# Gate rows of the matrix memory prepared two tiles ahead, and the weight sums of the down-projection issued behind the bank's sum

## The chip, the cores and the metric

The kernel runs on one core of a Trainium2 chip. The metric is the device time of one execution in microseconds. Before the change it is 2307.58 us, the median of 3 runs (2306.45 to 2310.1).

## What is computed

One encoder layer over 2048 prompt tokens and 128 sample tokens, D_MODEL = 1024, all in float32. A combined input projection feeds two groups of heads, an mLSTM matrix memory (4 heads of 128) and a sliding-window attention; their outputs go through one output projection and a norm, and a gated convolutional feed-forward network with D_FF = 2816 follows. Cut to what the change touches:

```python
def trunk_layer(x, pos, C0, n0, m0, k_cache, v_cache, conv_prev, mchunk, w_in, ...):
    qm, km, vm, om, ip, fp, qa, ka, va = split_in(x @ w_in)
    ...
    hm, C1, n1, m1 = mlstm_chunkwise(qm, km, vm, logi, logf, C0, n0, m0, mchunk)
    hm = (og * head_norm(hm, g_mlstm_norm)).reshape(B, T, M_WIDTH).astype(x.dtype)
    ...
    mix = jnp.concatenate([hm, ha], axis=-1) @ w_out
    h = layer_norm(DEEPNORM_ALPHA * x + mix, ln1_g, ln1_b)
    f, conv_rows = conv_ffn(h, conv_prev, w_up, w_conv, b_conv, w_down)
    y = layer_norm(DEEPNORM_ALPHA * h + f, ln2_g, ln2_b)

def step(carry, inp):          # of mlstm_chunkwise, one chunk
    C, n, m = carry
    b = jnp.cumsum(lf, axis=-1)
    inter = b + m[..., None]
    dmat = jnp.where(causal, b[..., :, None] - b[..., None, :] + li[..., None, :], -jnp.inf)
    mt = jnp.maximum(inter, jnp.max(dmat, axis=-1))
    w_inter = jnp.exp(inter - mt)
    s = jnp.einsum('bhld,bhsd->bhls', qc, kc) * jnp.exp(dmat - mt[..., None])
    num = w_inter[..., None] * jnp.einsum('bhld,bhde->bhle', qc, C) + jnp.einsum('bhls,bhse->bhle', s, vc)
    ...
```

## The kernel before

The work is cut into tiles of 128 tokens: 16 of the prompt (0 to 15) and one of the sample. It runs in four stages: the input projection (up to about 640 us), the output projection (to about 940 us), the up-projection of the feed-forward network (to about 1840 us) and the down-projection. The dense products of all stages use a fast matrix product with seven products for eight (Strassen's), so a product is named (b, g, s): block of tiles b, group of columns g, step s of the seven. Every fp32 operand is split into a high and a low half, and three matmuls are made for one.

In the input projection a product (b, g, s) fills one of three PSUM banks A, B and C. Behind it `i_after` empties banks: ACT copies A or B into a tile `zev` (L813, L816, L824), and in steps 5 and 4 the inner function `add` makes DVE add bank C to `zev` (L828 or L830): "the bank's sum". The next product into a bank cannot begin before its copy is done. The order of steps in a block is 1, 7, 6, 2 and then, for a group, 5, the next group's 1, 3, 4, then the next group's 6, 7, 2.

Between the dense products, two chains run tile by tile from about 280 us on: the matrix memory (`m_chain`) and the attention (`a_chain`). They are generators. `Chains.weave` advances a planned clock by the cost of each dense piece and steps a chain when its planned time has come: `yield cost, wait, banks` says how much TensorE time the step took, how long to stay away, and how many of the five rotating PSUM banks (`bank`) must be planned free. This fixes the order of TensorE's instructions. The order on DVE, ACT, POOL and SP is made by a scheduler from the order in which the program issues them and its own estimates; `issue_after(x)` puts what is issued under it behind `x` on x's engine. Each engine works through its list strictly in order.

Steps of one tile t of the matrix memory, with their lines before the change:

- `m_rows(t)`: two transposes of the gates into a bank `pgr` (L1057, L1058), then seven small DVE instructions on 4 partitions: two scans (`r_b` L1136, `r_M` L1138), `ay` L1137 and L1068, the row `nmrow` (L1140, L1141) and `mc` L1144.
- `m_spread(t, 0)` writes the row to memory (`zrow<-nmrow`, L1150); `m_spread(t, 1)` reads it back to all 128 partitions (`nm<-zrow`, L1153). Both are DMAs on SP's queue.
- `m_tile`: `m_cols` transposes `ay` (bank `pcol`) and copies it to `col` (L1079); `m_masked` makes `dt` from `nm` (L1175); `m_emt` (L1084); `m_inter`, four exponentials of `nm` to the weights `wi` (L1187); `m_exps`, four of `dt` (L1181); scores; `sd` (L1198), `kw` (L1272); then the banks `pnum` (L1282) and `pcu` (L1290).
- `m_norm`: statistics and `hn` on DVE (L1222), then `mr`, three instructions on `mq` (L1225 to L1227), and a power on POOL (L1228). `m_scaled`: `ms` on DVE (L1233) and four scalings of `hn` on ACT (L1235). `m_out`: four transposes of `hn` into the bank `pht` (L1245).

Before the change the rows of tile t+1 are made inside tile t, right behind its columns, and spread in its next two steps. `m_inter` depends on `nm` alone.

`d_sums(k, step)` prepares sums of the down-projection's weights, eight times in the second half of the input projection and three times in the output projection: step 0 loads two tiles `txy<-wdn` (L897, L898), step 1 makes four DVE subtractions on them (L903 to L906), step 2 stores them (`zt<-txy`, L908, L909).

Of the kernel before, what the change touches and what calls it, by code (L numbers as in the profile page):

```python
# [10 lines left out]
AF = mybir.ActivationFunctionType  # L11
# [193 lines left out]
class Prog:  # L205
# [416 lines left out]
    def i_dense(self):  # L622
# [18 lines left out]
        for q in (2, 4):  # L641
            for _ in range(2 + (q == 2) * 2):
# [18 lines left out]
        passages = [{1: ["load"], 7: ["t3", 7], 6: ["t2", 6], 3: [3, "t4"], 4: ["b12", "t1"]},  # L661
                    {1: ["load"], 6: ["t3"], 7: [7, "t2"], 5: [6], 3: [3, "t4"], 4: ["b12", "t1"]}]
        sums = 0
        after = None
        for item in self.items:
            if after:

                after[0] -= 1
                if after[0] == 3:
                    self.logs_of(after[1] - 1)  # L670
                if after[0] < 0:
                    self.i_done = after[1]
                    after = None
            self.chains.hold = item[0] == "t" and item[1] > 0
            if item[0] == "t":
                _, b, ti, e = item
                if ("g", e, 3) not in self.wu:
                    self.advance()
                if b not in self.gates:
                    self.gates[b] = self.tp.tile([P, 5, 8], F32, name="gates", tag="gates", bufs=2)  # L680
                ps = self.bank([P, 512], "pg") if ti == 4 or e < 0 and ti % 2 == 0 else self.ib[ti % 2 * 2]
                yield from self.i_direct(b, ti, e, ps)
                self.i_keys(b, ti, ps)
                if ti == 1 and b:
                    if b + 1 < nb:
                        self.x_steps(b + 1, 1, 2)
                    else:
                        self.release(4)
                    after = [6, b + 1]
                elif ti == 3 and b or ti == 4:  # L690
                    self.release(4)
                elif item in begin:
                    self.x_steps(0, *begin[item])
                    for e in self.x_room.values() if ti == 2 else ():
                        e[1] = True
                if ti == 3 and b or ti == 4:
                    self.x_steps(b, 4)
                    if b:
                        self.x_steps(b, 5)
                self.advance()  # L700
                continue
            _, b, g, s = item
            if item not in self.wu:
                self.advance()
            yield from self.i_product(b, g, s)
            del self.wu[item]
            self.release(2)
            if self.trans and s != 4:
                self.i_transposes()
            behind = self.i_after(b, g, s)  # L710
            if (b, g, s) == (0, 0, 7):
                self.t_setup()
            if b and (g, s) == (1, 6):
                self.rope_load(IBLOCKS[b][0], 2)
            if g == last and b + 1 < nb:
                if s == 7:
                    self.rope_load(IBLOCKS[b + 1][2], 2)
                for x in passages[b > 0].get(s, ()):
                    if x == "load":
                        self.spare = True  # L720
                        self.x_load(b + 1, 1, 2, 3, 4)
                    else:
                        self.x_steps(b + 1, x)
            if (b, g, s) == (0, last, 4):
                self.x_steps(1, 1, 2)
                after = [6, 1]
            if g == last and b + 1 == nb and s in (7, 5, 2, 3):
                self.x_pair(0, (7, 5, 2, 3).index(s))
            with self.tc.issue_after(behind) if behind and b == 0 else nullcontext():
                self.advance()  # L730
                self.x_steps(0, *begin.get(item, ()))
                if item == ("p", 0, 0, 2):
                    self.x_single(4)

            if b >= nb // 2 and g < last:

                steps = (6, 2, 5) if g == last - 1 else (6, 5, 3)
                if s in steps:
                    self.d_sums(sums, steps.index(s))
                    sums += s == steps[2]  # L740
        self.sums = sums
        self.logs_of(nb - 1)
        self.chains.hold = False
# [77 lines left out]
    def i_after(self, b, g, s):  # L821
# [3 lines left out]

        def add(u):
            if g < 2:
                V.scalar_tensor_tensor(u, C, KSCALE, u, op0=ALU.mult, op1=ALU.add)  # L828
            else:
                V.tensor_add(u, C, u)  # L830
        if s == 1 and g == 0:
            return nc.scalar.copy(B, A).ins
        elif s == 6:
# [247 lines left out]

    def m_emt(self, col):
        emt = self.work("emt", [P, MH], bufs=2)
        self.nc.scalar.activation(emt, col[:, 36:40], AF.Exp)  # L1084
        return emt

    def place(self, t, blocks=IBLOCKS):
# [8 lines left out]
    def m_chain(self):  # L1096
# [3 lines left out]
        pend = None  # L1100
        self.rows = {}
        there = lambda t: t < NPT and self.i_done > self.place(t)[0]
        for t in range(NPT):
            while not there(t):
                yield 0, 500
            if pend is None:
                self.m_rows(t)
                self.m_spread(t, 0)
                self.m_spread(t, 1)
# [4 lines left out]
            hn = self.m_norm(*(yield from self.m_tile(t, *pend, *self.rows.pop(t))))  # L1114
            pend = None
            yield 950, 3000, 1
            self.m_scaled(hn)
            if there(t + 1):
                if t + 1 not in self.rows:
                    self.m_rows(t + 1)  # L1120
                    self.m_spread(t + 1, 0)
                    self.m_spread(t + 1, 1)
                pend = self.m_load(t + 1, *self.place(t + 1)),
            yield 150, 6800, 1
            self.m_out(t, hn[0])
            self.chains.done["m"] = t
        nc.sync.dma_start(self.a["m_p"], self.mc)
        nc.sync.dma_start(self.a["cn_p"], self.C)

    def m_rows(self, t):  # L1130
# [14 lines left out]
        self.rows[t] = [i, nm]  # L1145

    def m_spread(self, t, step):
        nc, z = self.nc, self.zrow[t]
        if step == 0:
            self.behind_pe(nc.sync.dma_start(z.rearrange("o (h m) -> (o h) m", h=MH), self.rows[t][1]))  # L1150
            return
        self.rows[t][1] = nm = self.work("nm", [P, MH, 129], bufs=2)
        self.behind_pe(nc.sync.dma_start(nm.rearrange("p h m -> p (h m)"), z.to_broadcast([P, MH * 129])))  # L1153

    def m_load(self, t, b, ti):
# [95 lines left out]
    def m_tile(self, t, load, i, nm):  # L1251
# [3 lines left out]
        col = self.m_cols(i)  # L1255
        with self.tc.issue_after(self.colcopy.ins):
            dt = self.m_masked(nm[:, :, :P], self.mcau)
        ahead = t + 1 < NPT and self.i_done > self.place(t + 1)[0]
        if ahead:
            self.m_rows(t + 1)  # L1260
        yield 330, 2800
        emt = self.m_emt(col)
        wi = self.m_inter(nm)
        self.m_exps(dt, col)
        yield 0, 5000, 2
        if ahead:
# [5 lines left out]
        V.tensor_mul(kw, kt, dt[:, :, P - 1:P].to_broadcast([P, MH, P]))  # L1272
        nc.gpsimd.tensor_mul(qk[:, 0:4], qk[:, 0:4], wi)
# [953 lines left out]
```

## Time and profile before

| | us |
|---|---|
| median of 3 runs | 2307.58 |
| the profiled execution, its own time | 2307.89 |
| its span in the trace | 2305.7 |
| TensorE (PE) busy | 2266.6 |
| VectorE (DVE) busy | 1808.2 |
| ScalarE (ACT) busy | 1306.8 |
| GpSimd (POOL) busy | 225.5 |

The matmul engine is busy almost throughout, so the time is read from the places where it isn't: a row of the timeline gives start, duration, engine, line, output<-input, and in square brackets the idle time of the engine before it with what ended that. A row of the view of waits gives who waited for whom, the total in us, the number of times and the longest. The 2.2 us between the profiled execution's time and its span lie outside the trace.

### The profile page before, as it was taken

To read this page: it belongs to the slowest core of one execution; us is meant where nothing else is said; L and a number is where in the kernel's file an instruction comes from. 1 tells how busy PE (TensorE), PEld (TensorE's weight loads), DVE (VectorE), ACT (ScalarE), POOL (GpSimd) and SP (SyncE) were. 2 spreads that over 40 slices of the span, in tenths; PEclk is the share of its full clock that TensorE was granted. 3 is DMA by queue.
4 is the path that set the end of the run, shared out by engine and by line. 5 is a ranking of instruction groups with operands and counts; after the bars stand their busy time and mean duration, and the time that the engine had idled before them with its cause. 6 is when DMAs were issued, how large, how long until landed. Compare 5 with 4: busy or idle time off the path is not lost.

```text
span 2305.7 us, 39752 instructions
## 1 busy us (share of the span) xinstructions
PE 2266.6 (98%) x14329; PEld 2086.1 (90%) x14329; DVE 1808.2 (78%) x3157; ACT 1306.8 (57%) x2465; POOL 225.5 (10%) x289
## 2 busy tenths in 40 slices
PE   8999999999999999999999999999999999999998
PEld 8999989898887778999999999999999988888887
DVE  8777686787789888987788666778766787796897
ACT  5453466676765665555556455555554644654753
POOL 0001001101122121200002000002000000000100
PEclk9999999999999999999999999999999999999999
DMA  7898999899986767787777889888998786656753
GB/s 279 299 322 287 297 308 328 295 303 332 320 278 237 241 220 248 282 322 282 275 270 263 282 309 322 308 305 270 328 292 260 240 286 225 240 196 225 242 188 110
DMA packets 299797, 629.23 MB, mean 273 GB/s; under 512 B 47373, under 2 KB 140625, under 8 KB 299601
## 3 DMA queue, kind: packets, MB, share of 16 engines
q1 hardware_dynamic: 298736, 623.55, 79.1%
q10 hardware_dynamic: 864, 3.15, 0.4%
q8 instruction: 113, 1.85, 0.3%
q14 instruction: 84, 0.68, 0.1%
HBM read 456.01 MB, written 170.59 MB: 272 GB/s over the span
## 4 chain that ended last, share of the span: by engine, by line
PE 78%; DVE 10%; DMA 6%; ACT 3%; issue 2%; SPq 0%; POOL 0%; DVEq 0%; ACTq 0%; POOLq 0%
PE dps L1931 18%; PE fup L1931 18%; PE dps L758 11%; PE dps L2135 6%; PE fht L2135 6%; PE fup L2135 5%; PE dps L232 2%; PE dps L233 2%; PE dps L234 2%; DMA txy<-wdn 2%; DVE w L228 2%; PE dps L783 1%; DMA w<-zws 1%; PE psx L767 1%; PE ppo L1420 1%
## 5 line engine op out<-in xcount | busy, mean ns | idle before, releaser
L1931 PE MATMUL dps<-hh,uw 128*128 128x384 f32 (+1 forms) x1848 | 477.5, 327 | 5.4 <-DVE u L1964 2.6
L1931 PE MATMUL fup<-hh,uw 128*128 128x384 f32 (+1 forms) x1848 | 476.4, 326 | 0.0
L1979 DVE SCALAR_TENSOR_TENSOR cc<-u,cw,cc 128x768 f32<-128x768 f32 (+1 forms) x264 | 257.7, 978 | 125.0 <-ACT cc L1977 121.6
L1931 PEld LDWEIGHTS dps<-hh,uw 128*128 128x128 f32 x1848 | 329.2, 188 | 7.9 <-DVE u L1964 3.2
L1931 PEld LDWEIGHTS fup<-hh,uw 128*128 128x128 f32 x1848 | 329.3, 188 | 0.0
L1931 PE MATMUL fup<-hl,uw 128*128 128x384 f32 (+1 forms) x924 | 301.3, 326 | 0.2 <-DVE hl L228 0.2
L1931 PE MATMUL dps<-hl,uw 128*128 128x384 f32 (+1 forms) x924 | 301.0, 326 | 0.0
L758 PE MATMUL dps<-w,oh 128*128 128x256 f32 x1344 | 252.1, 283 | 4.6 <-DMA w<-zws 2.2
L758 PEld LDWEIGHTS dps<-w,oh 128*128 128x128 f32 x1344 | 210.1, 188 | 17.1 <-issue 9.3
L228 DVE TENSOR_TENSOR w<-wraw,w 128x1024 fp32r<-128x1024 f32 (+1 forms) x155 | 185.8, 1202 | 50.4 <-ACT w L227 48.0
L227 ACT CAST uw<-wraw 128x1024 fp32r<-128x1024 f32 x126 | 123.2, 981 | 173.4 <-PE dps L2135 104.1
L227 ACT CAST w<-wraw 128x1024 fp32r<-128x1024 f32 (+1 forms) x155 | 155.0, 1005 | 88.9 <-PE dps L758 44.3
L228 DVE TENSOR_TENSOR uw<-wraw,uw 128x1024 fp32r<-128x1024 f32 x126 | 142.5, 1131 | 63.9 <-ACT uw L227 63.8
L758 PE MATMUL dps<-w,ol 128*128 128x256 f32 x672 | 187.2, 279 | 0.0
L1977 ACT ACTIVATE cc<-u,cw 128x768 f32<-128x768 f32 (+1 forms) x132 | 131.9, 1000 | 95.6 <-DVE u L1973 92.6
L758 PE MATMUL dps<-oh,w 128*128 128x256 f32 x896 | 167.0, 282 | 7.8 <-ACT zev L824 3.9
L1931 PEld LDWEIGHTS fup<-hl,uw 128*128 128x128 f32 x924 | 173.5, 188 | 1.1 <-DVE hl L228 1.1
L1931 PEld LDWEIGHTS dps<-hl,uw 128*128 128x128 f32 x924 | 173.5, 188 | 0.0
L2135 PE MATMUL fup<-uw,fu 128*128 128x512 f32 x726 | 169.3, 389 | 0.1
L2135 PEld LDWEIGHTS fup<-uw,fu 128*128 128x128 f32 x726 | 136.1, 188 | 28.7 <-ACT fht L2142 0.5
L2135 PE MATMUL dps<-uw,fu 128*128 128x512 f32 x660 | 160.9, 389 | 0.1
L758 PEld LDWEIGHTS dps<-oh,w 128*128 128x128 f32 x896 | 139.7, 188 | 14.1 <-ACT zev L824 4.5
(346 smaller groups left out, 4563.6 us busy)
## 6 DMA issues: line engine op xcount, KB each, us to landing
uw<-zw SPq DMA_DIRECT2D x176, 512.0 KB
zw<-uw SPq DMA_DIRECT2D x88, 512.0 KB
w<-zws SPq DMA_DIRECT2D x72, 512.0 KB
wv<-wup SPq DMA_DIRECT2D x66, 512.0 KB
wraw<-wi SPq DMA_DIRECT2D x62, 512.0 KB
wraw<-zt SPq DMA_DIRECT2D x60, 512.0 KB
wraw<-wdn SPq DMA_DIRECT2D x45, 512.0 KB
wraw<-wo SPq DMA_DIRECT2D x40, 512.0 KB
```

What stands on the lines that cost most here:

```text
L227: nc.scalar.copy(hi, src)
L228: nc.vector.tensor_sub(lo, src, hi.bitcast(F32))
L232: mm(out, ah, bh, start=start, stop=False)
L233: mm(out, ah, bl, start=False, stop=False)
L234: self.mark = mm(out, al, bh, start=False, stop=stop)
L758: self.mark = mm(o, l, r, start=s in (1, 7) and c == k == i == 0, stop=k == 3 and i == 2, skip_group_check=True)
L767: mm(o, x[:, k], w[:, k], start=s == 1 and k == i == 0, stop=s in (2, 4) and k == 3 and i == 2, skip_group_check=True)
L783: mm(o, x, w, start=k == i == 0, stop=k == KD - 1 and i == 2, skip_group_check=True)
L1931: mm(ps, l[:, k], r[:, k], start=s in (1, 7) and k == 0 and i == 0, stop=k == 3 and i == 2, skip_group_check=True)
L1977: S.activation(c[:, v], u[:, v, 2:2 + n], AF.Identity, bias=w[3], scale=w[2])
L1979: V.scalar_tensor_tensor(c[:, v], u[:, v, i:i + n], w[i], c[:, v], op0=ALU.mult, op1=ALU.add)
L2135: mm(ps, l[:, k, c], r[:, k], start=s in (1, 4, 7) and u == 0 and k == 0 and i == 0, stop=u == nu - 1 and k == n - 1 and i == 2, skip_grou ...
```

## The change

The rows of tile t+2 are now made at the end of tile t, behind `m_scaled`; their write to memory is issued behind `m_out(t)`, and the read back to all partitions in the middle of tile t+1, behind `m_exps`. A flag in `self.rows` says whether the row has been spread. A tile whose rows are not there yet gets them at once, as before (`at_once`). `m_inter` is put behind `emt`, so the weights come behind the columns. The planned cost of the step after `m_cols` goes from 330 to 180. `d_sums` follows a table: the load one or more products earlier or at the same product, the subtractions mostly one product later (at step 1 of the next group) and behind the last bank's sum.

```diff
+        sum_at = {(0, 7): 0, (1, 1): 1, (0, 3): 2, (1, 6): 0, (2, 1): 1, (1, 3): 2,
+                  (2, 6): 0, (3, 1): 1, (2, 3): 2, (3, 6): 0, (3, 2): 1, (3, 5): 2}
...
-            if b >= nb // 2 and g < last:
-
-                steps = (6, 2, 5) if g == last - 1 else (6, 5, 3)
-                if s in steps:
-                    self.d_sums(sums, steps.index(s))
-                    sums += s == steps[2]
+            if b >= nb // 2 and (g, s) in sum_at:
+                step = sum_at[g, s]
+                with self.tc.issue_after(self.added.ins):
+                    self.d_sums(sums, step)
+                sums += step == 2
...
         def add(u):
             if g < 2:
-                V.scalar_tensor_tensor(u, C, KSCALE, u, op0=ALU.mult, op1=ALU.add)
+                self.added = V.scalar_tensor_tensor(u, C, KSCALE, u, op0=ALU.mult, op1=ALU.add)
             else:
-                V.tensor_add(u, C, u)
+                self.added = V.tensor_add(u, C, u)
...
+        def at_once(t):
+            if t not in self.rows:
+                self.m_rows(t)
+                self.m_spread(t, 0)
+                self.m_spread(t, 1)
...
             self.m_scaled(hn)
             if there(t + 1):
-                if t + 1 not in self.rows:
-                    self.m_rows(t + 1)
-                    self.m_spread(t + 1, 0)
-                    self.m_spread(t + 1, 1)
+                at_once(t + 1)
                 pend = self.m_load(t + 1, *self.place(t + 1)),
+            ahead = there(t + 2) and t + 2 not in self.rows
+            if ahead:
+                self.m_rows(t + 2)
             yield 150, 6800, 1
             self.m_out(t, hn[0])
+            if ahead:
+                self.m_spread(t + 2, 0)
...
         with self.tc.issue_after(self.colcopy.ins):
             dt = self.m_masked(nm[:, :, :P], self.mcau)
-        ahead = t + 1 < NPT and self.i_done > self.place(t + 1)[0]
-        if ahead:
-            self.m_rows(t + 1)
-        yield 330, 2800
+        yield 180, 2800
         emt = self.m_emt(col)
-        wi = self.m_inter(nm)
+        with self.tc.issue_after(self.emtcopy.ins):
+            wi = self.m_inter(nm)
         self.m_exps(dt, col)
+        if t + 1 in self.rows and not self.rows[t + 1][2]:
+            self.m_spread(t + 1, 1)
         yield 0, 5000, 2
-        if ahead:
-            self.m_spread(t + 1, 0)
...
         yield 950, 4000, 4
-        if ahead:
-            self.m_spread(t + 1, 1)
```

How it moves instructions is seen in the engines' lists. (In the change's list, line numbers are higher by 1 to 7: L1194 is the old L1187, L1240 the old L1233.) ACT's list at the end of tile 0, before:

```order
L816 COPY zev<-dps 128x512
L1187 ACTIVATE wi<-nm 128x128 x4
L227 CAST w<-wraw 128x1024
L1235 ACTIVATE hn<-hn,ms 128x128 x4
L824 ACTIVATE zev<-dps 128x512
L1415 COPY pth<-ppt 128x512 x2
```

The same place now:

```order
L817 COPY zev<-dps 128x512
L1242 ACTIVATE hn<-hn,ms 128x128 x4
L825 ACTIVATE zev<-dps 128x512
L227 CAST w<-wraw 128x1024 x2
L1418 COPY pth<-ppt 128x512 x2
```

The four weights of tile 1 stood between two copies of banks and ahead of tile 0's `hn`; now they stand further down, behind the columns of their own tile:

```order
L1085 ACTIVATE emt<-col 128x4
L853 COPY dps<-dps 128x512
L1430 COPY mixa<-ppo 128x512
L1194 ACTIVATE wi<-nm 128x128 x4
L1188 ACTIVATE dt<-dt,col 128x128 x4
```

DVE's list at the norm of tile 0 (`mq`, `ms`) and the second set of weight sums (`txy`), before:

```order
L1225 TENSOR_TENSOR mq<-bmv,mr 128x4
L1226 TENSOR_TENSOR mq<-mq,mr 128x4
L1227 TENSOR_SCALAR mq<-mq 128x4
L903 TENSOR_TENSOR txy<-txy 128x512
L1233 TENSOR_TENSOR ms<-ms,mr 128x4
L228 TENSOR_TENSOR w<-wraw,w 128x1024
L904 TENSOR_TENSOR txy<-txy 128x512
L828 SCALAR_TENSOR_TENSOR zev<-dps,zev 128x512
```

The same place now; `txy` is the first set of sums here:

```order
L1232 TENSOR_TENSOR mq<-bmv,mr 128x4
L1233 TENSOR_TENSOR mq<-mq,mr 128x4
L1143 SCALAR_TENSOR_TENSOR r_b<-pgr,k_seg 4x128
L1234 TENSOR_SCALAR mq<-mq 128x4
L1144 TENSOR_TENSOR ay_765<-pgr,r_b 4x128
L1240 TENSOR_TENSOR ms<-ms,mr 128x4
L1145 SCALAR_TENSOR_TENSOR r_M<-k_seg,mc,ay_765 4x128
L1147 TENSOR_SCALAR nmrow<-r_M 4x128
L1069 SCALAR_TENSOR_TENSOR ay_765<-r_b,r_M 4x128
L1151 TENSOR_TENSOR mc<-r_b,r_M 4x1
L1143 SCALAR_TENSOR_TENSOR r_b<-pgr,k_seg 4x128
L1148 COPY nmrow<-mc 4x1
```

The rows of tile 1 and of tile 2 now stand in and behind the tail of tile 0's norm, ahead of the bank's sum L829 and of the four subtractions, which follow it. All four subtractions of the earlier set, which stood some forty rows higher among the attention's reductions, have moved down to here.

More of the change, by code (lines that the diff above doesn't have):

```diff
@@ L1083, in m_emt @@
         emt = self.work("emt", [P, MH], bufs=2)
-        self.nc.scalar.activation(emt, col[:, 36:40], AF.Exp)
+        self.emtcopy = self.nc.scalar.activation(emt, col[:, 36:40], AF.Exp)
         return emt
@@ L1106, in m_chain @@
             if pend is None:
-                self.m_rows(t)
-                self.m_spread(t, 0)
-                self.m_spread(t, 1)
+                at_once(t)
                 pend = self.m_load(t, *self.place(t)),
@@ L1113, in m_chain @@
                 yield 0, 1000, 2
-            hn = self.m_norm(*(yield from self.m_tile(t, *pend, *self.rows.pop(t))))
+            hn = self.m_norm(*(yield from self.m_tile(t, *pend, *self.rows.pop(t)[:2])))
             pend = None
@@ L1144, in m_rows @@
         V.tensor_add(self.mc, bc[:, P - 1:P], M[:, P - 1:P])
-        self.rows[t] = [i, nm]
+        self.rows[t] = [i, nm, False]
     def m_spread(self, t, step):
@@ L1151, in m_spread @@
             return
-        self.rows[t][1] = nm = self.work("nm", [P, MH, 129], bufs=2)
+        self.rows[t][1:] = nm, _ = self.work("nm", [P, MH, 129], bufs=2), True
         self.behind_pe(nc.sync.dma_start(nm.rearrange("p h m -> p (h m)"), z.to_broadcast([P, MH * 129])))
```

## The prediction

> **What bounds the kernel now.** First the busy time of the engines by stretch; the columns are start and end, length, busy us of PE, PEld, DVE, ACT and POOL, the granted clock, the share of the DMA engines and GB/s. The change touches the stretch from 310 us, where the chains run beside the input projection, to 940 us.
>
> ```profile
> 310.00:640.00 330.00, 318.52 (x2636) 291.12 (x2635) 248.47 (x756) 231.14 (x606) 37.46 (x36) 0.99 0.93 316
> 640.00:940.00 300.00, 297.37 (x1630) 236.46 (x1630) 265.21 (x609) 186.28 (x443) 71.81 (x43) 1.00 0.72 240
> ```
>
> PE is busy for 318.52 of 330 us and for 297.37 of 300. No matmul is removed, so all there is to win is PE's idle time, 11.5 + 2.6 = 14.1 us, 0.6% of the run. Next, what PE waited for in the first stretch, then in the second:
>
> ```profile
> PE dps L758 <- ACT zev L824: 3.7, 3, 2.5
> PE dps L783 <- DVE zev L830: 2.1, 1, 2.1
> PE dps L758 <- DMA w<-zws: 0.9, 2, 0.8
> PE dps L758 <- ACT zev L816: 0.9, 1, 0.9
> PE pnum L1282 <- DVE sd L1198: 0.9, 1, 0.9
> PE dps L758 <- DVE zev L830: 0.8, 1, 0.8
> PE pgr L1057 <- ACT pth L1415: 0.8, 1, 0.8
> ...
> PE pht L1245 <- ACT hn L1235: 1.7, 2, 1.0
> ```
>
> Most of it is a bank not emptied in time (L816, L824, L830). ACT and DVE have time to empty it on average, 231 and 248 us of 330; they are late where their lists stand still. Why they do, from their own waits in the first stretch:
>
> ```profile
> ACT wi L1187 <- DMA nm<-zrow: 20.7, 7, 5.1
> ACT sc L1386 <- DVE amx L1379: 17.7, 10, 2.6
> DVE ms L1233 <- POOL ms L1228: 8.6, 8, 1.7
> DVE txy L903 <- DMA txy<-wdn: 6.5, 5, 2.3
> DVE txy L904 <- DMA txy<-wdn: 4.5, 2, 3.9
> ```
>
> ACT stands 20.7 us for `nm` and DVE 11.0 us for `txy`. These are the change's targets. But 31.7 us of standing lists cost PE little: the timeline shows where. PE first, then ACT and DVE.
>
> ```profile
> 314.20 0.49 PE L1282 MATMUL pnum<-v,sd 128*128 128x129 f32 x2 [0.87 <-DVE sd L1198]
> 319.23 0.39 PE L758 MATMUL dps<-oh,w 128*128 128x256 f32 x1 [0.67 <-ACT zev L824]
> 323.15 0.39 PE L758 MATMUL dps<-oh,w 128*128 128x256 f32 x1 [0.92 <-ACT zev L816]
> 330.14 0.39 PE L758 MATMUL dps<-oh,w 128*128 128x256 f32 x1 [2.55 <-ACT zev L824]
> ...
> 325.97 1.28 ACT L1187 ACTIVATE wi<-nm 128x128 f32<-128x128 f32 x4 [2.87 <-DMA nm<-zrow]
> 328.33 1.28 ACT L1235 ACTIVATE hn<-hn,ms 128x128 f32<-128x128 f32 x4
> 329.52 0.58 ACT L824 ACTIVATE zev<-dps 128x512 f32<-128x512 f32 x1
> ...
> 322.50 0.83 DVE L1222 SCALAR_TENSOR_TENSOR hn<-pnum,bmv,og 128x128 f32<-128x128 f32 x3
> 325.08 0.17 DVE L1227 TENSOR_SCALAR mq<-mq 128x4 f32<-128x4 f32 x1
> 327.53 0.69 DVE L903 TENSOR_TENSOR txy<-txy 128x512 f32<-128x512 f32 x1 [2.29 <-DMA txy<-wdn]
> 328.14 0.15 DVE L1233 TENSOR_TENSOR ms<-ms,mr 128x4 f32<-128x4 f32 x1
> ```
>
> Around 330 us both targets meet: ACT waits for `nm` to 325.97, then for `ms`, which stands on DVE behind a subtraction that waits for `txy` to 327.53. Only then comes `hn`, and behind it the copy L824 for which PE has stood 2.55 us. The four gaps make 0.87 + 0.67 + 0.92 + 2.55 = 5.0 us. The other place is at 410 us:
>
> ```profile
> 409.85 0.69 DVE L904 TENSOR_TENSOR txy<-txy 128x512 f32<-128x512 f32 x1 [3.92 <-DMA txy<-wdn]
> 414.77 0.39 PE L758 MATMUL dps<-w,oh 128*128 128x256 f32 x1 [0.73 <-ACT zev L813]
> 419.67 0.38 PE L758 MATMUL dps<-w,oh 128*128 128x256 f32 x1 [0.52 <-ACT zev L824]
> ```
>
> DVE stands 3.92 us, the columns behind it come late, ACT's exponentials too, and with them two copies: 1.25 us on PE.
>
> **The change part by part.** One row of the grouped view for each kind carries the durations of `d_sums` and `m_rows` (count, total us, mean ns, idle before):
>
> ```profile
> L903 DVE TENSOR_TENSOR txy<-txy 128x512 f32<-128x512 f32 x11 | 7.5, 683 | 6.5 <-DMA txy<-wdn 6.5
> L1138 DVE TENSOR_TENSOR_SCAN r_M<-k_seg,mc,ay 4x128 f32<-4x128 f32 x14 | 6.9, 490 | 0.3
> L1136 DVE TENSOR_TENSOR_SCAN r_b<-pgr,k_seg 4x128 f32<-4x128 f32 x14 | 5.7, 404 | 0.0
> L1068 DVE SCALAR_TENSOR_TENSOR ay<-r_b,r_M 4x128 f32<-4x128 f32 x14 | 3.9, 281 | 0.3
> L1137 DVE TENSOR_TENSOR ay<-pgr,r_b 4x128 f32<-4x128 f32 x14 | 3.8, 274 | 0.2
> L1140 DVE TENSOR_SCALAR nmrow<-r_M 4x128 f32<-4x128 f32 x14 | 3.0, 213 | 0.3
> ```
>
> A set of four subtractions is 4 x 0.68 = 2.7 us of DVE. The rows of a tile are 0.49 + 0.40 + 0.28 + 0.27 + 0.21 = 1.65 us, and some 1.9 with the two on 4x1, which I take at 0.14 each as an estimate below the 0.21. Nothing of it is added or removed; all of it moves.
>
> *At 313 to 330 us: -4.1.* The first set of sums moves behind the bank's sum, so three of its subtractions (2.0 us) no longer stand ahead of `sd`. DVE reaches `sd` at about 311.4 instead of 313.46, before PE wants it: 0.87 goes. ACT follows DVE there (it waited 17.7 us for `amx` in ten places), so its copies come up to 2.0 us earlier, more than 0.67 and than 0.92: both go. At the last gap, `mq` (its last instruction ended at 325.25) ends 2.7 us earlier and, with `r_b` (0.40) ahead of it, at 322.9; the weights are out of the way. From there to the end of a free power on POOL is 1.1 us (to 326.35 by the POOL row below), and `ay` fits into that, so `ms` can follow at 324.0. By the rows above `hn` begins 0.2 later, L824 1.2 after that, and it takes 0.58: it ends near 326.0. PE, 2.46 us ahead by the first three gaps, is there at 330.14 - 2.55 - 2.46 = 325.1: 0.9 of 2.55 stays. So 5.0 - 0.9 = 4.1; at the worst, if ACT keeps its pace, 1.4 (the last gap only by the time that `ms` waited), and 5.0 at the best.
>
> *At 414 and 419 us: -1.0.* This fourth set keeps its products (load at (3, 6), subtractions at (3, 2)), but it comes further back in DVE's list, behind the columns, and its two loads next to each other on SP. I take 1.0 of 1.25; 0 if the tile lands as late as it did.
>
> *The rows at the end of tile 0: +0.3.* Tiles 1 and 2 both get theirs here, with two banks `pgr`. The second one takes the bank of the first `pnum`, which is free after L1222, at 323.3 in this trace and 2.7 earlier by the above. The transposes stand behind the same dense matmuls that begin at 321.4 here, 319 by the same count. Between 0 and 1.9 us; 0.3 for a small overlap. `nm` for tile 1 starts later than before: its rows were made near 287 and now at 323.
>
> ```profile
> SPq L1153 <- DMA zrow<-nmrow: 3.3, 2, 2.4
> ...
> 325.33 1.02 POOL L1228 TENSOR_TENSOR ms<-mq,mhalf 128x4 f32<-128x4 f32 x1 [7.96 <-PE ppt L1414]
> ```
>
> With the read right behind the write, SP's queue stands for the landing, 2.4 us at the longest, and the weight loads behind it (`wraw`, `txy`) stand too. That costs nothing while the splits have a tile in hand; without that cover up to 2.4. The read itself took some 5.6 us (to 325.97). So `nm` is there near 334, and the weights behind the columns want it some 6 us later. For tiles 2 to 15 a whole tile lies between write and use: ACT's 20.7 us go.
>
> *All other rows: 0.* Thirteen tails of the norm get the row instructions of tile t+2. `ms` waits there for POOL anyway (8.6 us in eight places), which covers 0.67 us of `r_b` and `ay`; without the cover it is `hn` that comes late, the slow rival below. The weights come up to 1.3 us ahead of `dt`'s exponentials; `sd` takes those 3 us and more later, so I cost it at nothing.
>
> [...] A row, first: on DVE `amx` on 4 columns took 1.26 us while POOL's multiplication ran, against 0.13 alone.
>
> ```profile
> 308.08 1.29 POOL L1273 TENSOR_TENSOR qk<-qk,wi 128x512 f32<-128x512 f32 x1 [38.70 <-PE pscore L1193]
> 308.13 1.26 DVE L1379 SCALAR_TENSOR_TENSOR amx<-amx,nsink 128x4 f32<-128x4 f32 x1
> 313.33 0.13 DVE L1379 SCALAR_TENSOR_TENSOR amx<-amx,nsink 128x4 f32<-128x4 f32 x1
> ```
>
> [...]
>
> *Sum.* -4.1 - 1.0 + 0.3 = -4.8 against the profiled execution, whose own time is 2307.89 (2305.7 of span and 2.2 around it): 2303.1. It stands 0.3 above the median of the runs, 2307.58, so the forecast is 2302.8 for the median, with 2298 to 2306 for this case alone: the first term's ends less the smaller ones', and 2 us for gaps that shift.
>
> **The rivals.**
>
> *Everything catches up.* If both standing lists were behind the late copies at 459 us and later too (L830 with 2.1 and 0.8), all 11.5 us of the first stretch go: 2296.1. For it: a list that never stands has slack. Against: before 459 us DVE was busy, not waiting. Chance 0.12.
>
> *The gaps form again.* The chains' places shift by 4 to 8 us against the dense work, and the 5.2 us of gaps that have neither `nm` nor `txy` behind them (11.5 - 5.0 - 1.3) are drawn anew; at twice that the gain is gone: 2307.58 - 4.8 + 5.2 = 2308.0, give or take 3. DVE, with 248 of 330 and 265 of 300 us, is near enough to the bound for it. Chance 0.16.
>
> *The norm's tail becomes the bound: slower.* Place: `ms`, then `hn` on ACT, thirteen times; `hn` stands directly ahead of a bank's copy in ACT's list (as at 328.33 and 329.52), and `pht` already waited for it, 1.7 us in two places. Price: 0.67 us (two instructions ahead of `ms`) to 1.65 (five), say 1.0, in each tail that PE feels, 13 us; less the 4.8 gained, 2315.8. It decides from 0.72 us a tail on, where 13 x 0.72 = 9.4 eats the gain and 4.6 more. For it: the list shows the row instructions there. Against: it also shows 1.2 us casts gone from several of these places. Chance 0.24.
>
> **How the numbers follow.** The forecast has 0.48. A measurement of this kernel tells some 0.2%, 4.6 us, from no change: faster is below 2303.0, slower above 2312.2. Of the forecast's 0.48, 0.29 lies below 2303.0 and 0.19 above. Faster: 0.29 + 0.12 = 0.41. Same: 0.19 + 0.13 of the second rival + 0.02 of the slow one = 0.34. Slower: 0.22 + 0.03 of the second = 0.25. The range reaches from the catching-up rival, 2295, to the slow one's price, 2316, which leaves out half of that rival and little else.
>
> **What would show it.** Right: no wait of `wi` for `nm` on ACT, waits of `txy` on DVE under 4 us in all, PE without the four gaps of 313 to 330 us but for under 1 us, and idle on PE below 7 us in the first stretch. The first term is wrong if `sd` or L824 still end gaps of 2 us near 330. The cover is wrong if `pht` waits more than 1.7 us for `hn` from 640 us on, or if `hn` delays copies. The whole is wrong if PE's idle in the first stretch stays above 10 us although both DMA waits are gone.

## The result: slower by 0.35%, and the profile after

The changed kernel takes 2317.91 us (median of 22 runs) beside 2309.77 us for the kernel before (22 runs): a ratio of 1.0035, 95% interval 1.0028 to 1.0041, some 8 us slower. The forecast was 4.8 us faster. The profiled execution has a span of 2312.8 us, 7.1 more than the one before.

Busy time by stretch after the change, columns as in the prediction:

```profile
310.00:640.00 330.00, 311.94 (x2596) 287.26 (x2595) 243.48 (x735) 229.71 (x602) 39.47 (x36) 0.99 0.90 305
640.00:940.00 300.00, 294.89 (x1611) 233.27 (x1611) 258.76 (x613) 181.85 (x432) 70.92 (x43) 1.00 0.73 248
940.00:1840.00 900.00, 895.76 (x5461) 892.82 (x5461) 686.40 (x927) 497.32 (x846) 76.42 (x173) 1.00 0.83 291
```

TensorE (PE) stands 18.1 us in the first chain stretch instead of 11.5, and 5.1 instead of 2.6 in the second; from 940 to 1840 us nothing differs (895.73 of 900 before). What PE waited for from 310 to 640 us, then ACT and DVE (total, times, longest):

```profile
PE dps L784 <- DVE zev L831: 6.2, 2, 4.3
PE dps L759 <- ACT dps L853: 3.8, 3, 1.7
PE dps L759 <- ACT zev L825: 3.5, 3, 2.4
PE dps L759 <- DMA w<-zws: 2.6, 1, 2.6
...
ACT hn L1242 <- DVE ms L1240: 20.4, 9, 4.6
...
DVE txy L904 <- DMA txy<-wdn: 3.1, 2, 2.6
DVE txy L905 <- DMA txy<-wdn: 2.7, 2, 2.1
```

Both waits at which the change aims are smaller: `wi` no longer waits for `nm` at all (20.7 us before), `txy` waits 5.8 us instead of 11.0. But ACT now stands as long for `ms`, 20.4 us. Before it was:

```profile
ACT hn L1235 <- DVE ms L1233: 4.5, 5, 1.8
```

And PE has new gaps behind copies and bank sums, and one of 2.6 us for weights `w` read back from `zws`.

**The clock.** One thing the prediction had no term for shows in the windows. Four windows of the kernel after and three of the kernel before; the granted clock is the third number from the end:

```profile
455.00:460.00 5.00, 5.00 (x45) 5.00 (x44) 3.27 (x11) 5.00 (x14) 0.10 (x1) 1.00 0.98 348
460.00:465.00 5.00, 0.71 (x6) 0.49 (x5) 5.00 (x16) 3.71 (x8) 0.00 (x0) 1.00 0.80 243
465.00:469.00 4.00, 3.97 (x20) 3.97 (x21) 4.00 (x10) 1.05 (x1) 0.25 (x1) 0.57 0.98 279
469.00:474.00 5.00, 5.00 (x44) 5.00 (x43) 4.10 (x7) 3.37 (x7) 2.13 (x1) 1.00 1.01 348
```

```profile
325.00:330.00 5.00, 2.60 (x24) 2.40 (x22) 2.68 (x6) 3.89 (x11) 1.02 (x1) 1.00 1.01 387
330.00:335.00 5.00, 4.86 (x36) 3.75 (x38) 3.95 (x7) 3.91 (x8) 0.00 (x0) 1.00 0.82 239
462.00:466.00 4.00, 4.00 (x23) 4.00 (x22) 4.00 (x6) 3.10 (x10) 0.00 (x0) 0.57 1.06 332
```

Behind the gap of 4.32 us at 460.7 us the clock is halved for 3.4 us, and 20 matmuls go through in 4 us instead of some 35: 1.7 us more. So this gap is paid twice. Whether one is, is not read from its length: in the kernel before, the gap of 2.55 us at 327.6 us was followed by full clock, and one of 2.08 us at 459.0 us by a halved one. From 150 to 160 us, ahead of everything that was changed, PE stands 2.7 to 3.4 us in each of six profiles, and three things follow: full clock in the kernel before and in the changed one (a gap of 2.67 us in both), 3.4 us of half clock with the sums alone and with the rows, weights and cost 180 alone, 6.8 us in the change with cost 330 and in the change with late rows. Over the runs, the mean granted clock is 0.9956 after (22 runs) and 0.9968 before (31 runs beside the first experiments); 0.0012 of 2310 us is 2.8 us. By this estimate that is about a third of the loss. The rest should be idle time: in the two profiles PE stands 9.1 us longer from 310 to 940 us, and 2.2 us less ahead of 310 us.

### The profile page after: what moved, and what is told of

Read it like the earlier page. It is cut to its first block, busy times and chain, and to the rows that moved or that the text cites. A ratio compares the mean times of both kernels' runs of the same rounds, so it can differ in the third digit from the quotient of the medians.

```text
span 2312.8 us, 39749 instructions
## 1 busy us (share of the span) xinstructions
PE 2267.0 (98%) x14329; PEld 2089.3 (90%) x14329; DVE 1804.7 (78%) x3157; ACT 1307.3 (57%) x2465; POOL 228.3 (10%) x289
## 4 chain that ended last, share of the span: by engine, by line
PE 73%; DVE 7%; issue 2%; DMA 2%; ACT 2%; POOL 0%; SPq 0%; DVEq 0%; ACTq 0%; POOLq 0%
PE dps L1934 19%; PE fup L1934 19%; PE dps L2138 6%; PE dps L759 6%; PE fht L2138 5%; PE fup L2138 5%; PE dps L232 2%; PE dps L233 2%; PE dps L234 2%; PE ppo L1423 1%; DVE uw L228 1%; PE psc L1374 1%; PE ppt L1417 1%; DMA w<-zws 1%; DVE fu L228 1%
```

## The experiments

Each ran in five rounds beside the kernel before, and the ratio is to those runs. "The plan" is the planned clock of `Chains.weave`, which fixes TensorE's list, "late rows" is the rows of tile t+2 made behind `m_out` instead of ahead of it.

| kernel | ratio | 95% interval |
|---|---|---|
| sums alone | 1.0024 | 1.0013 to 1.0034 |
| rows, weights and cost 180 alone | 1.0016 | 1.0007 to 1.0026 |
| the change, cost 330 | 1.0034 | 1.0022 to 1.0046 |
| the change, late rows | 0.9992 | 0.9982 to 1.0003 |
| the change, rows behind `ms` on DVE | 1.0031 | 1.0020 to 1.0042 |
| late rows, plan of the change | 1.0033 | 1.0020 to 1.0045 |
| rows in the tail, plan of late rows | 1.0005 | 0.9996 to 1.0014 |
| late rows, old sums | 0.9963 | 0.9951 to 0.9976 |
| before, norm's wait 2000 | 1.0087 | 1.0073 to 1.0102 |
| late rows, sets 3 and 4 old | 1.0002 | 0.9993 to 1.0011 |
| late rows, old sums, `wi` free | 1.0016 | 1.0005 to 1.0027 |
| before, `wi` behind `emt` | 1.0000 | 0.9989 to 1.0010 |
| late rows, new table only | 0.9977 | 0.9966 to 0.9987 |
| late rows, second set behind the sum | 1.0002 | 0.9990 to 1.0014 |
| late rows, later block behind the sum | 0.9984 | 0.9973 to 0.9995 |
| rows in the tail, plan of late rows, old sums | 1.0003 | 0.9991 to 1.0014 |

### Taking the change apart

The kernel before with the new `sum_at` and `issue_after(self.added.ins)`, and nothing else:

> The kernel before with the new table of the weight sums alone (loads, subtractions behind the bank's sum, stores); rows and weights as before. Three theories. The norm's tail: the loss comes from the rows of tile t+2 in the norm's tail, so this kernel has none of it and only the gain of the sums: ratio to the kernel before 0.998 to 1.000, PE idle in 310 to 640 us at most 11 us. The sums themselves: their new places put casts and bank sums late: ratio 1.002 or more, with gaps of PE behind the bank's sum on DVE. Gaps redrawn: any change of the lists moves PE's idle by some microseconds either way, without a part that owns the loss: ratio anywhere from 0.997 to 1.003, and the parts do not add up to the whole.

The change with the old sums:

> The change without the table of the sums: rows two tiles ahead, weights behind the columns, planned cost 180, but the weight sums at their old products. The norm's tail: the whole loss and the sums' gain missing: ratio 1.004 to 1.007. The sums themselves: the loss goes: ratio 1.000 or less. Gaps redrawn: anywhere from 0.998 to 1.005, and not the whole less the sums' part.

The change with one number put back:

```diff
-        yield 180, 2800
+        yield 330, 2800
```

> The change with the planned cost of the step behind the columns left at 330 instead of 180, all else as changed. The cost only shifts the chains' places against the dense products. The norm's tail and the sums: as the change, ratio 1.003 to 1.004, since neither the tail nor the sums move. Gaps redrawn: another set of gaps with another sum, ratio off the change's 1.0035 by 0.0015 or more either way.

The change with the rows made behind `m_out`:

```diff
             ahead = there(t + 2) and t + 2 not in self.rows
-            if ahead:
-                self.m_rows(t + 2)
             yield 150, 6800, 1
             self.m_out(t, hn[0])
             if ahead:
+                self.m_rows(t + 2)
                 self.m_spread(t + 2, 0)
```

> The change with the rows of tile t+2 made behind the transposes of hn (m_out) instead of ahead of them, so that their instructions stand behind the norm's tail on DVE. The norm's tail: the 8 us of loss go and the gain shows: ratio 0.998 to 1.000, and ACT's hn waits for ms 10 us in all in 310 to 640 us instead of 20.4. The sums: no change, ratio 1.0035. Gaps redrawn: a ratio off 1.0035 by 0.0015 or more, but with hn's wait for ms about as long as in the change.

Both halves are slower by themselves, 0.24 and 0.16%, together about the whole 0.35%. The planned cost does nothing (1.0034; 12 rows of TensorE's list differ). Late rows take the whole loss away: 0.9992. That is what a theory of mine, in which the rows in the norm's tail make `hn` and the copies behind it late, asked for, and I would have believed it but for one number: ACT's wait of `hn` for `ms` should have fallen to 10 us, and stayed at 16.1 (total, times, longest):

```profile
ACT hn L1241 <- DVE ms L1239: 16.1, 9, 2.8
```

Worked out from the rows of `hn` on DVE and `ms`, the time from the last `hn` to `ms`, summed over 17 tiles, is 77.9 us before and 72.1 after: the tail had not become longer at all.

### The norm's tail against the plan

Moving `m_rows` moves its instructions (two transposes on TensorE and seven on DVE), and also the request for its bank `pgr`, which the plan counts among its five rotating banks. Three kernels tell the two apart. The change with only DVE's rows put behind `ms`; TensorE's list is the change's in all 13882 rows:

```diff
             if ahead:
-                self.m_rows(t + 2)
+                with self.tc.issue_after(self.ms.ins):
+                    self.m_rows(t + 2)
```

> The change with the rows' DVE instructions put behind ms (issue_after ms), the transposes and the plan untouched: TensorE's list is the change's, instruction for instruction. The norm's tail (rows ahead of ms make hn and the copies behind it late): the loss goes, ratio 0.999 to 1.001, as with the rows behind m_out (0.9992). The plan (asking for the bank pgr at the end of the tile moves the chains' steps against the dense products, and the new places meet the bank sums badly): TensorE's list is the same, so the loss stays, ratio 1.002 to 1.005, with the gap of about 4 us near 460 us still there.

Late rows, the plan told of the bank where the change asks for it. `ask` is the plan's note of a bank, and `False` keeps `m_rows` from making it (the lines that hand the flag on are not shown):

```diff
             if ahead:
-                self.m_rows(t + 2)
+                self.chains.ask(HOLDS["pgr"])
             yield 150, 6800, 1
             self.m_out(t, hn[0])
             if ahead:
+                self.m_rows(t + 2, False)
```

> The rows are made behind m_out, but the plan is told of their bank at the change's place, so that TensorE's list is the change's but for the 28 transposes of the gates. The norm's tail: no row instruction is ahead of ms, so 0.999 to 1.001. The plan: as the change, 1.002 to 1.005, with a gap of 2 us or more near 323 and one of about 4 us near 460 us.

And the counterpart, rows in the tail, the plan told behind `m_out`:

```diff
             if ahead:
-                self.m_rows(t + 2)
+                self.m_rows(t + 2, False)
             yield 150, 6800, 1
             self.m_out(t, hn[0])
             if ahead:
+                self.chains.ask(HOLDS["pgr"])
```

> The counterpart: the rows stay in the norm's tail as in the change, but the plan is told of their bank behind m_out, so that TensorE's list is that of the kernel with late rows but for the 28 transposes. The norm's tail: as the change, 1.003 to 1.004. The plan: as the kernel with late rows, 0.998 to 1.0005, PE idle 12 to 14 us in 310 to 640 us.

All three go with the plan: 1.0031 and 1.0033 where TensorE's list is the change's (but for the 28 transposes of the gates in the second), 1.0005 where it is that of late rows, wherever the rows' instructions stand. What the plan moves is seen in one row for each kernel: the 16 `hn` instructions of tiles 1 to 4 on DVE, with the start of the first and of the last. The rows, in this order: before, the change, late rows with the change's plan, rows in the tail with the plan of late rows.

```profile
L1222 DVE SCALAR_TENSOR_TENSOR hn<-pnum,bmv,og x16: 312/341/351, 358.4 to 479.7; 128x128 f32<-128x128 f32 x16
L1229 DVE SCALAR_TENSOR_TENSOR hn<-pnum,bmv,og x16: 318/342/351, 353.4 to 464.0; 128x128 f32<-128x128 f32 x16
L1231 DVE SCALAR_TENSOR_TENSOR hn<-pnum,bmv,og x16: 315/340/351, 355.2 to 468.0; 128x128 f32<-128x128 f32 x16
L1231 DVE SCALAR_TENSOR_TENSOR hn<-pnum,bmv,og x16: 317/342/351, 360.7 to 481.0; 128x128 f32<-128x128 f32 x16
```

With the bank asked for at the end of the tile, the norm of tile 1 comes 5 us sooner than before, and that of tile 4 some 15 us. With late rows these instructions run from 359.7 to 480.4 us, about where they stood before. In the planner's own clock it begins at one place: the first step of tile 1 is let in 4.9 us sooner, and as tiles and products go on at one pace, the later steps of the matrix memory in the input projection keep a lead of 3.2 to 4.9 us, two of them 8 and 12 (numbers that the planner works with, no times of the chip). Where that lead hurts is seen at 460 us. DVE, the change first, then rows in the tail with the other plan:

```profile
461.14 1.22 DVE L593 TENSOR_TENSOR xr<-xr,wraw 128x1024 f32<-128x1024 f32 x1
462.28 0.86 DVE L1296 SCALAR_TENSOR_TENSOR C<-C,wi,pcu 128x129 f32<-128x129 f32 x3
463.05 0.24 DVE L1224 BATCH_NORM_AGGREGATE bmv<-bst 128x2 f32<-128x6 f32 x2
463.21 1.09 DVE L1229 SCALAR_TENSOR_TENSOR hn<-pnum,bmv,og 128x128 f32<-128x128 f32 x4
464.22 0.15 DVE L1230 TENSOR_TENSOR mr<-mr,emt 128x4 f32<-128x4 f32 x1
464.29 0.69 DVE L831 TENSOR_TENSOR zev<-dps,zev 128x512 f32<-128x512 f32 x1
```

```profile
461.12 1.21 DVE L593 TENSOR_TENSOR xr<-xr,wraw 128x1024 f32<-128x1024 f32 x1
462.25 0.68 DVE L831 TENSOR_TENSOR zev<-dps,zev 128x512 f32<-128x512 f32 x1
```

The norm of tile 4 has slid ahead of the bank's sum L831: 2.0 us of DVE for which the next block's first product waits. That product before, in the change, and in rows in the tail with the other plan:

```profile
461.06 0.39 PE L783 MATMUL dps<-w,oh 128*128 128x264 f32 x1 [2.08 <-DVE zev L830]
465.03 0.39 PE L784 MATMUL dps<-w,oh 128*128 128x264 f32 x1 [4.32 <-DVE zev L831]
462.99 0.39 PE L784 MATMUL dps<-w,oh 128*128 128x264 f32 x1 [1.60 <-DVE zev L831]
```

At 394.7 us it is ACT: tile 2's `hn` and the attention's copies stand ahead of the copy L853 (a gap of 1.75 us). Two more gaps near 603 and 635 us (1.45 and 1.89) stand behind the attention's exponentials on ACT and its reductions on DVE.

Is the plan alone enough? The kernel before with one number changed, which gives nearly the change's list on TensorE and touches neither rows nor weights nor sums:

```diff
-            yield 950, 3000, 1
+            yield 950, 2000, 1
```

> The kernel before with one number changed: the planned wait ahead of the norm's scaling is 2000 instead of 3000. Rows, weights and sums stay as they were; TensorE's list becomes the change's but for about 200 of 13882 rows, 60 of them the gate transposes. The plan (the places of the chains' steps make the loss): ratio 1.002 to 1.005, with gaps of 2 us or more near 323 and 460 us. If rows and weights have to move for the loss: 0.999 to 1.001.

PE's waits there from 310 to 640 us, and its busy time in that stretch:

```profile
PE dps L758 <- ACT dps L852: 6.7, 3, 4.4
PE dps L758 <- ACT zev L824: 6.3, 4, 2.8
PE dps L783 <- DVE zev L830: 5.0, 1, 5.0
...
310.00:640.00 330.00, 306.90 (x2470) 282.70 (x2468) 230.85 (x693) 214.32 (x562) 37.25 (x36) 0.95 0.89 293
```

It is slower by 0.87%, 20 us, more than the forecast of 1.002 to 1.005: 23.1 us of idle time in this stretch, with a granted clock of 0.95. So the place of the tiles is enough for a loss. That the change's other parts gave some of it back would explain why the change loses less; no run here separates this.

### What the sums cost, and what the rest is worth

Late rows with the old sums:

> Rows behind m_out as in the earlier kernel, and the weight sums at their old products. If the sums' new places cost what they cost alone (1.0024), this is 0.997 to 0.998 and beats both kernels. If they cost little by themselves and their ratio alone came from redrawn gaps and the clock, it stays within 0.001 of the kernel with late rows and new sums, 0.9992.

At 0.9963 this beats both kernels, and the sums cost 0.3% beside 0.9992. The kernels so far with new sums have a gap of 2 to 4.5 us between 429 and 439 us for `w` from `zws`, this one has none. The tiles `txy` share their buffers with the tiles `xr` of the next block. So I put the last two of four sets back:

```diff
-                  (2, 6): 0, (3, 1): 1, (2, 3): 2, (3, 6): 0, (3, 2): 1, (3, 5): 2}
+                  (2, 6): 0, (2, 5): 1, (2, 3): 2, (3, 6): 0, (3, 2): 1, (3, 5): 2}
...
-                with self.tc.issue_after(self.added.ins):
+                with self.tc.issue_after(self.added.ins) if sums % 4 < 2 else nullcontext():
```

> The kernel with late rows (0.9992 with all sums new, 0.9963 with all sums old), in which the first two of each four sets of weight sums follow the new table and the last two stand as before. If the later stores of the last two sets hold up the tiles xr that they share and bunch the loads ahead of 430 us: the gap of 4 us for w from zws near 430 us goes, and the ratio is 0.996 to 0.9975. If the first two sets cost it: 0.9985 to 1.000.

It missed: 1.0002, and the gap stayed (3.38 us at 428.7 us). The trace says why: each set loads into the tiles that the one before must first have stored, so the lateness of the first sets had reached the last, whose store went out at 420.1 us, as with all sets new (420.7; 404.4 with the old ones). Three kernels then took the sums apart by what stands behind the bank's sum:

```diff
-                with self.tc.issue_after(self.added.ins):
+                with self.tc.issue_after(self.added.ins) if COND else nullcontext():
```

all with late rows, and `COND` False (the table only), `sums % 4 == 1` (the second set of each four), and `sums >= 4` (the later block only).

> The kernel with late rows, in which the weight sums follow the new table but are not put behind the bank's sum. DVE's list is that of the kernel with late rows and old sums (0.9963) instruction for instruction, SP's differs in 8 rows: the table by itself moves nothing. If the placement behind the bank's sum is the whole cost of the sums: 0.995 to 0.9975. If the table's later products cost it: 0.9985 to 1.000.

> The kernel with late rows and the new table, in which only the second of each four sets of weight sums stands behind the bank's sum. On SP its store comes 25 rows later, and since each set loads into the tiles of the one before, the stores of the third and fourth set come later too, as with all sets behind. If the cost of the sums is the fourth store, on which the next x tiles wait with the weights w behind them on SP: 0.9985 to 1.0005, SP waits for zt 2 to 5 us ahead of L577, and PE has a gap of 2 us or more near 430 us for w from zws. If the cost lies in DVE's list (all subtractions behind the bank's sums): a quarter of it, 0.9965 to 0.9975.

> As the one before, but the four sets of the first block stand as in the table alone and the four of the second block stand behind the bank's sum. The fourth store: no gap near 430 us, and no x tiles wait behind the last set: 0.995 to 0.9975. DVE's list: half of the cost, 0.9975 to 0.9985.

The table alone costs nothing that shows (0.9977, its interval overlaps that of 0.9963). One set behind the sum brings all that the sums cost here (1.0002). SP's queue in that kernel, its wait ahead of L577, and PE's gap:

```profile
424.02 0.81 SPq L909 DMA_DIRECT2D zt<-txy  x1
424.88 0.43 SPq L910 DMA_DIRECT2D zt<-txy  x1
425.41 0.99 SPq L510 DMA_DIRECT2D w<-zws  x1
428.45 1.50 SPq L577 DMA_DIRECT2D xr<-xq  x2
430.04 1.09 SPq L510 DMA_DIRECT2D w<-zws  x1
...
SPq L577 <- DMA zt<-txy: 2.8, 2, 2.0
...
436.88 0.80 PE L759 MATMUL dps<-w,oh 128*128 128x256 f32 x2 [4.00 <-DMA w<-zws]
```

The load of `xr` needs the buffer that the fourth store is still reading; it stands at the head of SP's queue 2.8 us, and the weights `w` behind it reach PE 4 us late. In the change it is 4.4 us for L577. Without the first block's sets behind the sum the gap is gone, at 0.9984. That is not the 0.995 to 0.9975 that I expected if the store were the whole cost; it lies in the range for a cost in DVE's list. Its interval reaches from the table alone to all sets behind the sum, so the gap is shown to come from the store, but the split of the cost is not shown.

Late rows and old sums, with the weights no longer behind `emt` (the edit shown); and the kernel before with the weights behind `emt`, otherwise as it was (the opposite edit):

```diff
-        with self.tc.issue_after(self.emtcopy.ins):
-            wi = self.m_inter(nm)
+        wi = self.m_inter(nm)
```

> The kernel with late rows and old sums (0.9963), with the weights wi no longer put behind emt; TensorE's list is the same. If the gain comes from the rows being two tiles ahead, so that nm is there in time: 0.995 to 0.9975, no wait of wi for nm over 5 us in all. If it comes from the weights behind the columns: 0.999 to 1.000.

> The kernel before with the weights wi put behind emt and nothing else; TensorE's list is the kernel before's. If the gain of 0.37% comes from the weights standing out of the way: 0.996 to 0.998. If the rows two ahead are needed for it: 0.999 to 1.001, and ACT's wait for nm, 20.7 us, mostly turns into waits of hn for ms and of the weights for nm further down.

Without the weights' place the late rows are slower than before (1.0016), which neither theory had, and the weights' place alone does nothing (1.0000). The gain of 0.37% takes both. TensorE's list is the same in each pair, so this is not the plan. With the rows two ahead but the weights free, `wi` still stands for `nm`, for 11.8 us in all, and a gap of 3.17 us on PE at 533.8 us follows one of these waits:

```profile
ACT wi L1194 <- DMA nm<-zrow: 11.8, 7, 4.6
...
533.10 1.28 ACT L1194 ACTIVATE wi<-nm 128x128 f32<-128x128 f32 x4 [2.28 <-DMA nm<-zrow]
```

With the weights behind `emt` and the rows as before, no wait for `nm` is left; but `hn` now waits 21.6 us for `ms` instead of 4.5, and the gap near 330 us is 3.19 us instead of 2.55. So the 20.7 us of ACT's wait, the change's first target, were worth nothing that shows by themselves.

Last, rows in the tail with the other plan and the old sums, for whether the parts add up:

> Rows in the norm's tail as in the change, the plan told of their bank behind m_out, sums at their old places: what the change would be without its two found costs. If the parts add up (late rows and old sums 0.9963, rows in the tail 0.0013 more): 0.996 to 0.998, faster than the kernel before. If the gaps are merely drawn anew by each edit: anywhere from 0.996 to 1.002.

They don't: 1.0003 where 0.996 to 0.998 was expected. All seven kernels of this family side by side:

| place of the rows, plan | new sums | old sums |
|---|---|---|
| in the tail, the change's | 1.0035 | 1.0016 |
| late, the change's | 1.0033 | not run |
| in the tail, that of late rows | 1.0005 | 1.0003 |
| late, that of late rows | 0.9992 | 0.9963 |

The plan costs 0.30 and 0.41% with the new sums, but 0.13% with the old ones. The sums cost 0.19 and 0.29% in two pairs and 0.02% in the third. The rows' place costs 0.40% here, 0.13% with the new sums and 0.02% with the change's plan. What differs by 0.14% says little: late rows with old sums (0.9963) and with the new table only (0.9977) have the same lists on TensorE, DVE and ACT. DVE's tail is again not it (80.1 us from `hn` to `ms` over 17 tiles, 79.8 with late rows). PE's waits name the bank:

```profile
PE pgr L1060 <- DVE C L1299: 1.1, 1, 1.1
...
PE pk L1318 <- DVE ay L1147: 0.7, 1, 0.7
```

`pgr` waits for a bank that DVE still reads (L1299), and the attention's `pk` for the one that `ay` holds. These rows don't carry 9 us; the size of this part stays open.

## Why the prediction was wrong

**313 to 330 us, forecast -4.1: mis-sized.** The rows after:

```profile
319.28 0.27 PE L1058 MATMUL pgr<-ident,g 128*4 128x128 f32 x1 [0.19 <-DVE C L1296]
325.91 0.58 PE L759 MATMUL dps<-oh,w 128*128 128x256 f32 x1 [2.42 <-ACT zev L825]
...
324.10 1.28 ACT L1242 ACTIVATE hn<-hn,ms 128x128 f32<-128x128 f32 x4 [3.67 <-DVE ms L1240]
325.28 0.57 ACT L825 ACTIVATE zev<-dps 128x512 f32<-128x512 f32 x1
...
323.90 0.16 DVE L1240 TENSOR_TENSOR ms<-ms,mr 128x4 f32<-128x4 f32 x1 [0.88 <-POOL ms L1235]
```

With 0.32 at 311.5 and 0.42 at 316.1, gaps of 3.35 us stand where 5.0 stood: -1.7, the 0.19 of the rows' bank counted in. That `ms` came at 323.9, 324.0 by the forecast, is luck: the whole trace runs 1.84 us ahead here (`pscore` begins at 305.05, before at 306.89). On the clock of the trace before, PE was at the product at 325.3, as forecast (325.1), and `ms` came at 325.7, 1.7 too late. The mistake is the lead that I gave DVE, 2.0 us at `sd` and 2.7 at the norm. On that clock `sd` began at 312.9, only 0.55 sooner, and `pnum` and the norm behind it came no sooner than that. Three subtractions less stood ahead of `sd`, but further up DVE now stood 1.70 us for a cast on ACT, where before it had, among others, the rows of tile 1 to do:

```profile
292.15 1.23 DVE L228 TENSOR_TENSOR w<-wraw,w 128x1024 fp32r<-128x1024 f32 x1 [1.70 <-ACT w L227]
...
311.07 0.68 DVE L1205 TENSOR_TENSOR sd<-pscore,dt 128x512 f32<-128x512 f32 x1
```

And the half clock at the end of the gap, 325.4 to 328.9 us (the granted clock is 0.66 from 325 to 330 us), takes most of the 1.7 back. Two readings were off as well, without a term that rests on them: those rows of tile 1 were made at 290 to 294 us, not near 287, and ahead of `hn` near 328 us ACT made a cast to 328.19 and hardly waited for `ms`.

**414 and 419 us, forecast -1.0: right at its place, wrong in what the sums cost.** Both gaps are gone (1.25 us). I had the fourth set "further back in DVE's list" and thought of its columns only. Its store holds the next block's `xr`, SP's queue and `w` behind it: 2.56 us at 433 us where 1.3 us of small gaps stood. By the runs the sums cost 0.02 to 0.3%, by the kernel that they stand in, and the step that failed is the one that my own list asked for: a DMA that moves, and each queue that it is moved past.

**Rows of tiles 1 and 2, +0.3:** 0.19 us, counted above. **`nm`:** its wait is gone, as forecast.

**"All other rows: 0" failed.** From 310 to 940 us PE's idle time rose by 9.1 us; the two places above gave -1.7 and -1.2, so all other rows, the gap at 433 us among them, hold some +12 us where I had 0. The term had the rows' DVE instructions and the cover of `ms`; these cost 0.02 and 0.13% with the new sums, as the kernels with the rows behind `ms` and the two with exchanged plans show (with the old sums the rows' place costs 0.40%, for a reason that stays open). It left out that `m_rows` also asks for a bank, and that the plan turns this into another place for every later tile.

**The rivals.** *The gaps form again* was the right mechanism, with the right shift of some 4 us; I priced it by doubling the gaps that could be drawn anew, so that it only ate the gain. Measured, the shift costs 0.3 to 0.4% with the change's sums, 0.13% with the old ones, and 0.87% in the kernel before. *The norm's tail becomes the bound* came near in number (2315.8), but its mechanism is the one that fell: no row instruction ahead of `ms` was needed for the loss. *Everything catches up* (2296.1) did not happen, not even at 0.9963, the best that rows ahead and weights behind the columns gave when neither the plan nor the sums got in the way: in that kernel's profile PE still stands 9.2 us from 310 to 640 us, beside 11.5 before. Where the rest of its gain lies, its profile (the slowest of its five runs) does not show.

**What I said would show it** showed it: idle on PE above 10 us though both DMA waits are gone or halved, and `hn` ahead of copies. `r_M` met the power on POOL in one tail only, at 512.9 us: it took its usual 0.47 us, and the power 1.10 instead of 1.01. At 543.1 us `ay` ran its usual 0.28 us inside a power of 1.01 us. That the rows share these tails with the power cost this kernel nothing that shows.

## What to carry to other kernels

Where a planner places chains against dense work, a step that takes a bank is also an input to the plan: moving it can shift every later step, and that shift may be worth more than the stall that the move removes. So compare the matmul engine's list with the step's own instructions taken out; if it is the same, cost the instructions, and if not, look in the new list at what now stands ahead of each bank's copy. A wait that leaves an engine's list can stand again further down it, as the 20.7 us for `nm` did as 20.4 us for `ms`. Follow a moved store to whoever next uses its buffer, and to what stands behind that one in the queue.

## What the runs showed of the hardware

In the profiles before and after the change PE has thirteen gaps of 1.4 us or more. Within 1.6 us of the end of three of them (2.08, 2.42 and 4.32 us) 3.4 us at half clock begin, which are worth up to 1.7 us; the other ten, the longest 2.67 us, have full clock behind them. The mean granted clock of a kernel's runs is 0.9982 for the fastest kernel here and 0.9930 for the slowest; in between it does not order them (0.9978 at the ratio 1.0003, 0.9969 at 1.0016). At two places a DVE and a GpSimd instruction ran at the same time and one of them took longer: before the change `amx` on DVE took 1.26 us at 308 us beside a multiplication on GpSimd, 0.13 alone; after it, beside a subtraction of `txy` that had begun first, it was the power on GpSimd, 1.39 us at 391 us against 1.02 alone.
